# A hybrid convolution and RG-LRU layer: the first projection stage over half of the rows for two sets of seven column tiles, half sums kept in SBUF, and the statistics on two engines

## The chip, the core and the metric

The kernel runs on one core of one Trainium2 chip, in one launch. The metric is the device time of one execution in microseconds (us). Before the change it is 858.16 us, the median of three runs (857.1 to 858.53). PE is TensorE (matmuls), PEld its weight loads, DVE VectorE, ACT ScalarE, POOL GpSimd, and SP the engine that issues the DMAs.

## The reference, cut to what matters

```python
mod_lat = silu(c) @ w_ada + b_ada                  # shift, scale, gate for 512 latent tokens
mod_ctx = silu(c_ctx) @ w_ada + b_ada              # the same for 256 context tokens
hl = rmsnorm(x, norm_g) * (1 + sc_l) + sh_l        # (512, 2048)
hc = rmsnorm(ctx, norm_g) * (1 + sc_c) + sh_c      # (256, 2048)
bl, cl, ul, gl, vl, ql = split(hl @ w_in)          # six blocks of 1024 columns
vc = (hc @ w_in) block v
ya = bl * conv3(cl * ul) * silu(gl)                # rows of 64 tokens
xb = conv4(v) + b_conv_b                           # latent and context
# for both directions: a, b from two block diagonal products and sigmoids of xb,
# h = scan(a, b), the latent scan starting from the last context state
yb = (h_fwd + h_bwd) * silu(ql)
out = rmsnorm(x + gate * (concat(ya, yb) @ w_out), final_g)
```

All of it is float32. The kernel forms a float32 product from three passes: each operand is split into a rounded high part and the remainder (`hi`, `lo`), and `mm3` adds hi*hi, lo*hi and hi*lo.

## The kernel before, in words

The 2048 rows of `w_in` are 16 row tiles (k), its 6144 columns 48 column tiles of 128, named c0, u0, b0, g0 and so on, v0 to v7, q0 to q7. Tokens are the 512 columns of a matmul, and hidden rows are on the partitions.

**Start.** The 16 tiles of x arrive by DMA. ACT squares each one (L211), PE sums the squares over the partitions (L215), with a small matmul of ones behind each from k = 8 on (L218). The sums go through DVE and ACT to 1/rms, which PE transposes over all partitions (L230). `silu_c` (L129) takes a sigmoid on ACT at k = 8. `ada` (L199) multiplies silu(c) with four pieces of `w_ada` for one k; `ada_t` (L236) transposes the result and DVE makes the scale `gs` and shift `sh` of this k; `h_lat` (L252) makes `hi` and `lo` of the hidden row tile.

**First stage (L324).** It goes over all 16 row tiles k; at each k seven column tiles (A_TILES) get their three matmuls each, into seven PSUM banks that stay open for the stage. Between them stand the `ada`, `ada_t` and `h_lat` of the next k, so the stage makes the hidden tiles as it uses them. 2 MB of `w_ada` and 448 KB of `w_in` are loaded for each k.

**Second stage (L584).** A step s takes one half (8 row tiles) of one column tile: 24 matmuls, and 24 narrower ones (256 context tokens) more for a v tile. 82 steps do the other 41 tiles. At its head a step loads the piece for s + 3 and splits that for s + 2 (`split`, L71: `whi` on ACT, then `wlo` on DVE; three buffers each). A finished tile is worked up in the next step (`EV`). Lists by step number (`at`, L516) place all else behind the matmuls of a step: the context's squares and sums (`ctx_sq`, `ctx_stat`, `ctx_stat2`), its hidden tiles (`h_ctx`, L258: product on DVE, `hi` on ACT, `lo` on DVE), the RG-LRU of head tile m in seven steps (`l_prep`, `l_gate`, `l_ix`, `l_exp`, `l_mul`, then `l_sqrt` and `l_scan` in the next seven), the gate `gt_load` and `gt_acc`. Each engine runs its instructions in the order of the code.

**Last stage (L681).** 32 steps multiply y (split by `y_split`, L576) with `w_out`, whose piece DVE first multiplies by the gate (L316), and add x; the final norm ends it.

Of the kernel before, what the change touches and what calls it, by code (L numbers as in the profile page):

```python
# [14 lines left out]
D = 2048  # L15
# [14 lines left out]
for _n, _w in PCOLS:  # L30
# [5 lines left out]
A_TILES = [("c", 0), ("u", 0), ("b", 0), ("g", 0), ("c", 1), ("u", 1), ("b", 1)]  # L36
_REST = [("g", 1)] + [(n, m) for m in range(2, NM) for n in "cubg"]
N_FIRST = 3
BC_TILES = (_REST[:N_FIRST] + [("v", m) for m in range(NM)] + _REST[N_FIRST:]
            + [("q", m) for m in range(NM)])  # L40
NA = len(A_TILES)
W_OFF = {"b": 0, "c": 8, "u": 16, "g": 24, "v": 32, "q": 40}
N_BC = 2 * len(BC_TILES)
N_D = 32
N_GT = 32
NHC = 3
# [3 lines left out]
def tile_hybrid_layer(ctx, tc, xt, ct, xn, wada, wgt, bgt, wa_, wbc, wout, lruw, par, ident, fg, out):  # L50
# [11 lines left out]
    ctx.enter_context(tc.manual_schedule())  # L62
    s_a = ExitStack()
    ta = s_a.enter_context(tc.tile_pool(name="ta", bufs=2))
    pa = ctx.enter_context(tc.tile_pool(name="pa", bufs=6, space=PSUM))
# [96 lines left out]
    aux = pa.tile([128, 512], F32, name="bacc")  # L162
    acc = [pa.tile([128, 512], F32, name="bacc") for i in range(NA - 2)]
    accp = pa.tile([128, 2, 512], F32, name="plru", bufs=1)
    acc += [accp[:, 0, :], accp[:, 1, :]]
# [53 lines left out]
    ssum = ta.tile([128, T], F32, name="sq", bufs=4)  # L219
# [7 lines left out]
    ada(0, 0)  # L227
    ada(0, 1)
# [4 lines left out]
    ada(0, 2)  # L233
    ada(0, 3)
# [23 lines left out]
    def h_ctx(ks):  # L258
        for k in ks:
            nc.vector.scalar_tensor_tensor(xc[k], xc[k], gs[:, k, 1:2], cq["b"], op0=ALU.mult, op1=ALU.mult)  # L260
        for k in ks:
            hctx[k] = (hc.tile([128, TC], F32R, name="xchi", bufs=16 + NHC), hc.tile([128, TC], F32R, name="hclo"))
            nc.scalar.activation(hctx[k][0], xc[k], AF.Identity, bias=sh[:, k, 1:2])
        for k in ks:
# [3 lines left out]
    def ctx_sq(k):  # L268
        t = ta.tile([128, TC], F32, name="sqc", bufs=12) if k else const.tile([128, TC], F32, name="sqc0")
# [6 lines left out]
    def ctx_stat():  # L276
        ps = pa.tile([128, 512], F32, name="bacc")
# [7 lines left out]
    def ctx_stat2():  # L285
        ps = pa.tile([128, 512], F32, name="bacc")
# [5 lines left out]
    def main_a(k, j):  # L292
        hi, lo = wsp["a", k]
        s = slice(128 * j, 128 * j + 128)
        mm3(acc[j], hi[:, s], lo[:, s], hlat[k], T, k == 0, k == KT - 1)


    def piece_src(s):
        if s < N_BC:
            return wbc[s]  # L300
        return wout[s - N_BC]

# [15 lines left out]

    ada_t(0)
    h_lat(0)  # L320
    split_a(0)
    ada(1, 0)
    ada(1, 1)
    for k in range(KT):  # L324
        if k + 2 < KT:
            for p in range(4):
                load_ada(k + 2, p)
            load_wa(k + 2)
        else:
# [464 lines left out]
```

## Time and profile before

| | |
|---|---|
| median of three runs | 858.16 us |
| profiled execution | 858.19 us |
| its span, first to last instruction | 856.4 us |
| PE busy | 838.6 us, 98% |
| DVE, ACT, POOL busy | 493.5 us (58%), 376.6 us (44%), 89.1 us (10%) |
| granted PE clock, mean over the span | 0.993 of full |
| moved by DMA | 136.13 MB |

The span is what the trace covers; 1.8 us of the device time lie outside it. PE's busy time is modelled from its starts, so that the distance from one matmul's start to the next says more than its duration. A row of the timeline has start, duration, engine, line, operation, operands, how many instructions were merged (x), and in brackets how long the engine had been idle and what ended that.

### The profile page before, as it was taken

The page shows a single profiled execution, that of the slowest core. Times are in us where ns is not written, and L with a number is a line of the kernel's source. Part 1 is how long each engine was busy: PE and PEld are TensorE (multiplying, and loading weights), DVE is VectorE, ACT ScalarE, POOL GpSimd, SP SyncE. Part 2 cuts the span into 40 slices and gives each one's busy share as a digit, 9 for nine tenths or more (in the row PEclk, how much of TensorE's full clock was granted, in tenths as well). Part 3 has the DMA queues.
Part 4 walks back from the last instruction along what each step waited for, and adds up shares of the span by engine and source line. Part 5 has one row for each costly group of instructions (what it writes and reads, how often), then busy time and mean ns, then how long its engine had stood idle before and what let it go on. Part 6 is the DMA issues. An engine that isn't in the chain of part 4 may idle for free.

```text
span 856.4 us, 10577 instructions
## 1 busy us (share of the span) xinstructions
PE 838.6 (98%) x4202; PEld 665.3 (78%) x4202; DVE 493.5 (58%) x643; ACT 376.6 (44%) x478; POOL 89.1 (10%) x64
## 2 busy tenths in 40 slices
PE   7899999999999999999999999999999999999996
PEld 1466666888888888878888888887788888888784
DVE  0353434786355446394939585766465777454555
ACT  6322224451111024757576857475846443222234
POOL 0000001600000000202020202120202002020200
PEclk9899999999999999999999999999999999999998
DMA  9899998234222324244435443434223542323204
GB/s 341 341 326 333 352 357 291 103 120 139 82 99 82 116 86 159 99 131 152 143 116 164 145 159 122 161 123 135 74 99 141 204 171 102 120 74 113 84 0 197
DMA packets 41091, 136.13 MB, mean 159 GB/s; under 512 B 4561, under 2 KB 6865, under 8 KB 40401
## 3 DMA queue, kind: packets, MB, share of 16 engines
q1 hardware_dynamic: 41042, 135.46, 44.8%
q8 instruction: 33, 0.54, 0.3%
q14 instruction: 16, 0.13, 0.0%
HBM read 131.24 MB, written 4.19 MB: 158 GB/s over the span
## 4 chain that ended last, share of the span: by engine, by line
PE 93%; DVE 3%; ACT 1%; DMA 1%; issue 1%; SPq 0%; POOL 0%; ACTq 0%; DVEq 0%; POOLq 0%
PE bacc L78 21%; PE bacc L79 20%; PE bacc L80 20%; PE bacc L706 6%; PE bacc L708 6%; PE bacc L707 6%; PE bacc L201 4%; PE plru L78 1%; DMA xhi<-in_xt 1%; PE plru L454 1%; PE plru L79 1%; PE plru L80 1%; PE plru L706 1%; PE plru L708 1%; PE plru L707 1%; PE plru L456 1%
## 5 line engine op out<-in xcount | busy, mean ns | idle before, releaser
L78 PE MATMUL bacc<-xhi,whi 128*128 128x512 f32 x736 | 293.3, 399 | 1.6 <-ACT whi L73 1.6
L74 DVE TENSOR_TENSOR wlo<-raw,whi 128x1024 fp32r<-128x1024 f32 (+1 forms) x130 | 162.2, 1252 | 220.5 <-ACT whi L73 219.3
L79 PE MATMUL bacc<-xhi,wlo 128*128 128x512 f32 x736 | 288.1, 391 | 0.5 <-DVE wlo L74 0.5
L80 PE MATMUL bacc<-hlo,whi 128*128 128x512 f32 x736 | 287.7, 391 | 0.0
L73 ACT CAST whi<-raw 128x1024 fp32r<-128x1024 f32 (+1 forms) x130 | 134.3, 1035 | 246.3 <-PE bacc L80 127.2
L78 PEld LDWEIGHTS bacc<-xhi,whi 128*128 128x128 f32 x736 | 138.5, 188 | 37.2 <-issue 7.5
L80 PEld LDWEIGHTS bacc<-hlo,whi 128*128 128x128 f32 x736 | 138.6, 188 | 30.3
L79 PEld LDWEIGHTS bacc<-xhi,wlo 128*128 128x128 f32 x736 | 138.7, 188 | 28.3 <-DVE wlo L74 1.2
L706 PE MATMUL bacc<-whi,yhi 128*128 128x512 f32 x224 | 87.3, 390 | 0.3 <-DVE xr L639 0.3
L707 PE MATMUL bacc<-wlo,yhi 128*128 128x512 f32 x224 | 87.2, 389 | 0.0
L708 PE MATMUL bacc<-whi,ylo 128*128 128x512 f32 x224 | 87.1, 389 | 0.0
L464 POOL TENSOR_TENSOR li<-li,xb 128x768 f32<-128x768 f32 x16 | 30.9, 1933 | 393.5 <-ACT li L461 393.5
L460 ACT ACTIVATE lr<-plru,pt 64x768 f32<-64x768 f32 x32 | 28.8, 899 | 48.6 <-PE plru L457 41.7
L706 PEld LDWEIGHTS bacc<-whi,yhi 128*128 128x128 f32 x224 | 42.0, 188 | 9.4 <-DVE xr L639 0.8
L708 PEld LDWEIGHTS bacc<-whi,ylo 128*128 128x128 f32 x224 | 42.0, 188 | 8.8
L707 PEld LDWEIGHTS bacc<-wlo,yhi 128*128 128x128 f32 x224 | 42.0, 188 | 8.7
L504 DVE SCALAR_TENSOR_TENSOR gacc<-raw,cs,gacc 128x1024 f32<-128x1024 f32 x32 | 42.5, 1329 | 0.1
L316 DVE TENSOR_TENSOR raw<-raw,gacc 128x1024 f32<-128x1024 f32 x32 | 41.7, 1304 | 0.0
L80 PE MATMUL bacc<-hclo,whi 128*128 128x256 f32 x128 | 36.2, 283 | 0.0
L79 PE MATMUL bacc<-xchi,wlo 128*128 128x256 f32 x128 | 36.2, 283 | 0.0
L78 PE MATMUL bacc<-xchi,whi 128*128 128x256 f32 x128 | 36.1, 282 | 0.0
L201 PE MATMUL bacc<-rada,cs 128*32 128x256 f32 x512 | 35.1, 393 | 0.3 <-DVE mods L242 0.3
(158 smaller groups left out, 859.0 us busy)
## 6 DMA issues: line engine op xcount, KB each, us to landing
raw<-in_wbc SPq DMA_DIRECT2D x82, 512.0 KB, 3.2
rada<-in_wada SPq DMA_DIRECT2D x64, 512.0 KB, 5.7
raw<-in_wgt SPq DMA_DIRECT2D x32, 512.0 KB, 4.3
raw<-in_wout SPq DMA_DIRECT2D x32, 512.0 KB, 3.2
raw<-in_wa_ SPq DMA_DIRECT2D x16, 448.0 KB, 6.9
xhi<-in_xt SPq DMA_DIRECT2D x16, 256.0 KB, 4.9
xr<-in_xn SPq DMA_DIRECT2D x4, 1024.0 KB, 7.2
xchi<-in_ct SPq DMA_DIRECT2D x16, 128.0 KB, 3.7
```

Source lines behind the costliest of these rows:

```text
L73: nc.scalar.copy(hi[:, :n], raw[:, :n])
L74: nc.vector.tensor_tensor(lo[:, :n], raw[:, :n], hi[:, :n].bitcast(F32), op=ALU.subtract)
L78: nc.tensor.matmul(acc, wh, h[0][:, :n], start=first, stop=False, **kw)
L79: nc.tensor.matmul(acc, wl, h[0][:, :n], start=False, stop=False, **kw)
L80: nc.tensor.matmul(acc, wh, h[1][:, :n], start=False, stop=last, **kw)
L201: nc.tensor.matmul(aux[32 * j:32 * j + 32, 0:256], cs[:, 4 * p + j, :], rawa[g, p][:, j, :], start=p == 0, stop=p == 3, skip_group_check=True)
L316: nc.vector.tensor_tensor(r3, r3, g, op=ALU.mult)
L464: nc.gpsimd.tensor_tensor(lru["i", d], lru["i", d], xb[m], op=ALU.mult)
L504: nc.vector.scalar_tensor_tensor(gacc[:, s], gtq.pop(i), cs[:, k, 0:1], gacc[:, s], op0=ALU.mult, op1=ALU.add)
L706: nc.tensor.matmul(accs[t], yh[:, ts], hi[:, w], start=kk == 0, stop=False)
L707: nc.tensor.matmul(accs[t], yh[:, ts], lo[:, w], start=False, stop=False)
L708: nc.tensor.matmul(accs[t], yl[:, ts], hi[:, w], start=False, stop=kk == KT - 1)
```

## The change

The first stage covers only the first eight row tiles, for the same seven column tiles (now P_TILES). Their half sums are then copied out of PSUM into SBUF tiles (`part`), three by DVE and four by ACT. Seven other tiles (Q_TILES: c2, u2, b2, g2, c3, u3, b3) follow in single steps: steps 0 to 6 over the first eight row tiles, with the `ada`, `ada_t` and `h_lat` of k = 9 to 15 between their matmuls, steps 7 to 13 over the last eight. Steps 14 to 29 are the v tiles, steps 30 to 36 the second halves of P_TILES, to which DVE adds the half sums (`ev_part`), steps 37 to 88 the remaining 26 tiles. There are 89 steps for 82 before, and eight long steps of the first stage for 16. The matmuls of the projection are the same in number.

At the start DVE squares the odd x tiles, the matmuls of ones stand in groups (`warm`), all four `ada` of k = 0 come behind the transposes, and the weights of k = 0 are split before its `h_lat`. The context is loaded in step 6, squared in steps 7 to 9, summed at the end of step 10; its hidden tiles are made one at a time. The last LRU scan is in step 87 of 89 (79 of 82 before), and all six first `y_split` in step 88 (80 and 81 before).

```diff
+P_TILES = [("c", 0), ("u", 0), ("b", 0), ("g", 0), ("c", 1), ("u", 1), ("b", 1)]
+Q_TILES = [("c", 2), ("u", 2), ("b", 2), ("g", 2), ("c", 3), ("u", 3), ("b", 3)]
+_REST = ([("g", 1), ("g", 3)] + [(n, m) for m in range(4, NM) for n in "cubg"]
+         + [("q", m) for m in range(NM)])
+STEPS = ([(t, 0) for t in Q_TILES] + [(t, 1) for t in Q_TILES]
+         + [(("v", m), h) for m in range(NM) for h in range(2)]
+         + [(t, 1) for t in P_TILES] + [(t, h) for t in _REST for h in range(2)])
+S_V = 2 * len(Q_TILES)
...
+    def warm(n):
+        for _ in range(n):
+            nc.tensor.matmul(acc[0][:, :128], ones, ones, start=True, stop=True)
...
-        nc.scalar.activation(sq, xl[k], AF.Square)
+        if k % 2:
+            nc.vector.tensor_tensor(sq, xl[k], xl[k], op=ALU.mult)
+        else:
+            nc.scalar.activation(sq, xl[k], AF.Square)
...
-        if k >= 8:
-            nc.tensor.matmul(acc[0][:, :128], ones, ones, start=True, stop=True)
+    warm(3)
...
-    ada(0, 0)
-    ada(0, 1)
+    warm(4)
...
-    ada(0, 2)
-    ada(0, 3)
+    for p in range(4):
+        ada(0, p)
+    warm(2)
...
     ada_t(0)
+    warm(8)
+    split_a(0)
     h_lat(0)
-    split_a(0)
     ada(1, 0)
     ada(1, 1)
...
+    def main_p(k, j):
+        main_a(k, j)
+        if k == KH - 1:
+            part.append(ya.tile([128, T], F32, name="yA"))
+            if j % 2:
+                nc.vector.tensor_copy(part[j], acc[j])
+            else:
+                nc.scalar.copy(part[j], acc[j])
...
-    S_C0 = 2 * (N_FIRST + NM)
+    S_C0 = S_V + 2 * NM
...
-    at(3, h_ctx, range(0, 3))
-    at(4, h_ctx, range(3, 6))
-    at(4, h_ctx, range(6, 9))
-    at(5, h_ctx, range(9, 12))
-    at(5, h_ctx, range(12, 15))
-    at(5, h_ctx, range(15, 16))
+    for k in range(KT):
+        at(NA + k // 6, ctx_sq, k)
+        at(S_V - 3 + k // 6, h_ctx, [k])
+    at(S_V - 4, ctx_stat)
+    at(S_V - 3, ctx_stat2, first=True)
...
     for k in range(6):
-        at(S_Y + k // 3, lambda k=k: y_split(dp1[0], k))
+        at(S_Y, lambda k=k: y_split(dp1[0], k))
...
+    def ev_part(n, m, ps):
+        t = part[P_TILES.index((n, m))]
+        nc.vector.tensor_tensor(t, t, ps, op=ALU.add)
+        if n == "c":
+            cur["c"] = t
+        else:
+            EV[n](m, t)
...
+            if s < NA and k in (1, 3, 6):
+                h_ada(KH + 1 + s, {1: 0, 3: 1, 6: 2}[k])
...
+            if c < 2:
+                sets = (sets if c else []) + [[bank() for _ in range(2 if c else 4)]]
+                if c == 1:
+                    sets[1] += [pair[:, 0, :], pair[:, 1, :]]
+            accs = sets[c % 2]
```

`h_ada(k, j)` is the old `ada(k, 2)`, `ada(k, 3)` for j = 0, `ada_t(k)`, `h_lat(k)` for j = 1, and `ada(k + 1, 0)`, `ada(k + 1, 1)` for j = 2. `bank()` hands out six PSUM banks in turn, as the pool did.

The order on DVE where the context's hidden tiles are made, before: `xchi` is the product, `hclo` the remainder, which needs the `hi` that ACT makes from the product.

```order
L179 TENSOR_TENSOR rq_rc<-rq_rc,rq_uc 128x2
L74 TENSOR_TENSOR wlo<-raw,whi 128x1024
L260 SCALAR_TENSOR_TENSOR xchi<-xchi,gs,rinvC 128x256 x3
L265 SCALAR_TENSOR_TENSOR hclo<-xchi,sh 128x256 x3
L74 TENSOR_TENSOR wlo<-raw,whi 128x1024
L504 SCALAR_TENSOR_TENSOR gacc<-raw,cs,gacc 128x1024
L260 SCALAR_TENSOR_TENSOR xchi<-xchi,gs,rinvC 128x256 x3
```

The products stand in threes, so that ACT can work on the first while DVE makes the next. The same place on DVE now, in steps 11 and 12, with the numbers of the tiles:

```order
L531 SCALAR_TENSOR_TENSOR gacc_1349<-raw_1521,cs_132,gacc_1349 128x1024
L277 SCALAR_TENSOR_TENSOR xchi_1256<-xchi_1256,gs_161,rinvC_1572 128x256
L284 SCALAR_TENSOR_TENSOR hclo_1577<-xchi_1256,sh_162,xchi_1576 128x256
L277 SCALAR_TENSOR_TENSOR xchi_1258<-xchi_1258,gs_161,rinvC_1572 128x256
L284 SCALAR_TENSOR_TENSOR hclo_1583<-xchi_1258,sh_162,xchi_1582 128x256
L277 SCALAR_TENSOR_TENSOR xchi_1260<-xchi_1260,gs_161,rinvC_1572 128x256
```

Each remainder now stands right behind its own product; six such pairs stand between one `wlo` and the next (steps 11 and 12), four more behind that of step 13.

The order on DVE at the end of the second stage, before: `lt` to `xb` (L486 to L492) is the last scan, `sgt` and `xb` (L395, L396) the gate of a q tile, `raw` the multiplication of a `w_out` piece, `ylo` the split of y.

```order
L395 TENSOR_TENSOR sgt<-sgt,bacc 128x512
L396 TENSOR_TENSOR xb<-xb,sgt 128x512
L74 TENSOR_TENSOR wlo<-raw,whi 128x1024
L486 TENSOR_TENSOR lt<-lt,li 128x768
...
L492 TENSOR_TENSOR xb<-li 128x512
L316 TENSOR_TENSOR raw<-raw,gacc 128x1024
L74 TENSOR_TENSOR wlo<-raw,whi 128x1024
L395 TENSOR_TENSOR sgt<-sgt,bacc 128x512
L396 TENSOR_TENSOR xb<-xb,sgt 128x512
L580 TENSOR_TENSOR ylo<-yA,yhi 128x512 x3
```

Behind the scan stand the piece of the last stage's first step and the gate of q6. The same place now:

```order
L335 TENSOR_TENSOR raw<-raw,gacc 128x1024
L87 TENSOR_TENSOR wlo<-raw,whi 128x1024
L423 TENSOR_TENSOR sgt<-sgt,bank_86 128x512
L424 TENSOR_TENSOR xb<-xb,sgt 128x512
L513 TENSOR_TENSOR lt<-lt,li 128x768
...
L519 TENSOR_TENSOR xb<-li 128x512
L335 TENSOR_TENSOR raw<-raw,gacc 128x1024
L87 TENSOR_TENSOR wlo<-raw,whi 128x1024
L612 TENSOR_TENSOR ylo<-yA,yhi 128x512 x6
L423 TENSOR_TENSOR sgt<-sgt,bank_87 128x512
```

The scan has moved behind the gate of q6 and behind the first piece of the last stage, and the six splits behind the second piece.

## Rows read from the trace of the kernel before

**Rows 1.** The page's first section: busy us, share of the span, instructions, by engine.
```profile
PE 838.6 (98%) x4202; PEld 665.3 (78%) x4202; DVE 493.5 (58%) x643; ACT 376.6 (44%) x478; POOL 89.1 (10%) x64
```

**Rows 2.** What PE waited for: us in total, times, longest us.
```profile
PE plru L454 <- ACT li L461: 0.5, 1, 0.5
...
PE bacc L706 <- DVE xr L639: 0.3, 1, 0.3
```

**Rows 3.** Stretches of the start: busy us of each engine, granted clock, DMA.
```profile
30.00:31.00 1.00, 0.28 (x8) 0.00 (x0) 0.27 (x1) 0.70 (x2) 0.00 (x0) 1.00 0.95 340
...
34.00:36.00 2.00, 2.00 (x17) 0.60 (x16) 0.00 (x0) 0.00 (x0) 0.00 (x0) 0.50 0.96 390
```

**Rows 4.** The chain that ended last, at the start: start us, us, what.
```profile
15.02 0.97 PE plru L215 x2
15.99 0.42 PE bacc L218 x2
```

**Rows 5.** The timeline of the start.
```profile
12.75 0.23 ACT L130 ACTIVATE sg<-pt 128x32 f32<-128x32 f32 x1
...
23.00 0.69 DVE L220 COPY sq<-plru 128x512 f32<-128x512 f32 x1 [9.64 <-PE plru L215]
...
26.88 1.07 PE L201 MATMUL bacc<-rada,cs 128*32 128x256 f32 x16
...
28.44 0.44 PE L239 MATMUL bacc<-idt,sada 128*128 128x128 f32 x2 [0.49 <-ACT sada L205]
...
29.52 0.75 DVE L247 SCALAR_TENSOR_TENSOR xhi<-xhi,gs,rinvB 128x512 f32<-128x512 f32 x1
...
31.90 0.65 PE L78 MATMUL bacc<-xhi,whi 128*128 128x512 f32 x1 [1.62 <-ACT whi L73]
...
43.07 0.40 PE L78 MATMUL bacc<-xhi,whi 128*128 128x512 f32 x1
```

**Rows 6.** The timeline of DVE while the context's hidden tiles are made, and after.
```profile
174.28 1.28 DVE L260 SCALAR_TENSOR_TENSOR xchi<-xchi,gs,rinvC 128x256 f32<-128x256 f32 x3 [1.21 <-ACT rinvC L290]
...
190.56 0.48 DVE L260 SCALAR_TENSOR_TENSOR xchi<-xchi,gs,rinvC 128x256 f32<-128x256 f32 x1
191.67 0.48 DVE L265 SCALAR_TENSOR_TENSOR hclo<-xchi,sh 128x256 fp32r<-128x256 f32 x1 [0.64 <-ACT xchi L263]
...
193.76 0.68 DVE L380 TENSOR_TENSOR cutile<-ctile,bacc 128x512 f32<-128x512 f32 x1
...
196.43 1.28 DVE L504 SCALAR_TENSOR_TENSOR gacc<-raw,cs,gacc 128x1024 f32<-128x1024 f32 x1
```

**Rows 7.** The timeline of ACT at the same place.
```profile
191.13 0.51 ACT L263 ACTIVATE xchi<-xchi,sh 128x256 fp32r<-128x256 f32 x1 [1.06 <-DVE xchi L260]
191.54 1.04 ACT L73 CAST whi<-raw 128x1024 fp32r<-128x1024 f32 x1
```

**Rows 8.** The timeline of PE there: first matmuls of steps 4, 6 and 7.
```profile
173.54 0.48 PE L78 MATMUL bacc<-xhi,whi 128*128 128x512 f32 x1
...
184.52 0.39 PE L78 MATMUL bacc<-xhi,whi 128*128 128x512 f32 x1
...
192.83 0.40 PE L78 MATMUL bacc<-xhi,whi 128*128 128x512 f32 x1
```

**Rows 9.** The timeline of DVE at the end of the second stage.
```profile
659.93 0.95 DVE L486 TENSOR_TENSOR lt<-lt,li 128x768 f32<-128x768 f32 x1
...
666.22 1.22 DVE L316 TENSOR_TENSOR raw<-raw,gacc 128x1024 f32<-128x1024 f32 x1
668.69 1.23 DVE L74 TENSOR_TENSOR wlo<-raw,whi 128x1024 fp32r<-128x1024 f32 x1 [1.25 <-ACT whi L73]
...
671.93 1.89 DVE L580 TENSOR_TENSOR ylo<-yA,yhi 128x512 fp32r<-128x512 f32 x3
```

**Rows 10.** The timeline of ACT there.
```profile
667.60 1.05 ACT L73 CAST whi<-raw 128x1024 fp32r<-128x1024 f32 x1 [9.14 <-DVE raw L316]
...
676.08 1.66 ACT L579 CAST yhi<-yA 128x512 fp32r<-128x512 f32 x3
```

More of the change, by code (lines that the diff above doesn't have):

```diff
@@ L62, in tile_hybrid_layer, with bank @@
     ctx.enter_context(tc.manual_schedule())
+    ya = ctx.enter_context(tc.tile_pool(name="ya", bufs=9))
     s_a = ExitStack()
     ta = s_a.enter_context(tc.tile_pool(name="ta", bufs=2))
-    pa = ctx.enter_context(tc.tile_pool(name="pa", bufs=6, space=PSUM))
+    pa = ctx.enter_context(tc.tile_pool(name="pa", bufs=1, space=PSUM))
+    single = [pa.tile([128, 512], F32, name=f"bank{i}") for i in range(6)]
+    pair = pa.tile([128, 2, 512], F32, name="pair")
+    turn = [5]
+    def bank():
+        turn[0] += 1
+        return single[(turn[0] - 1) % 6]
     def raw_tile():
@@ L159, in softplus @@
         nc.vector.tensor_scalar(nsp8, w0, -LRU_C, None, op0=ALU.mult)
[L162 to L165, printed above, removed]
+    aux = single[5]
+    acc = single[:5] + [pair[:, 0, :], pair[:, 1, :]]
     cq = {}
@@ L276, in ctx_stat @@
     def ctx_stat():
-        ps = pa.tile([128, 512], F32, name="bacc")
+        ps = bank()
         for j in range(2):
@@ L285, in ctx_stat2 @@
     def ctx_stat2():
-        ps = pa.tile([128, 512], F32, name="bacc")
+        ps = bank()
         for j in range(2):
@@ L412, in ev_v @@
     def ev_v(m, ps, psc):
[L413 removed]
+        t = xbp.tile([128, TA], F32, name="xb")
         xb[m] = t
@@ L506, in gt_sum @@
     def gt_sum(j):
-        p = pa.tile([128, 512], F32, name="bacc")
+        p = bank()
         s = slice(512 * j, 512 * j + 512)
@@ L583, in tile_hybrid_layer @@
     load_piece(2)
-    for s in range(N_BC):
-        ti, half = divmod(s, 2)
-        n, m = BC_TILES[ti]
+    for s, ((n, m), half) in enumerate(STEPS):
+        if s < NA - 1:
+            for p in range(4):
+                load_ada(KH + 2 + s, p)
+        if s == NA - 1:
+            for k in range(KT):
+                load_xc(k)
+        if s == NA:
+            s_a.close()
+            xbp = ctx.enter_context(tc.tile_pool(name="xbp", bufs=8, reuse_waits="tile"))
+            gp = ctx.enter_context(tc.tile_pool(name="gp", bufs=1, reuse_waits="tile"))
+            tq[0] = s_c.enter_context(tc.tile_pool(name="tcx", bufs=1, reuse_waits="tile"))
+            gacc = gp.tile([128, D], F32, name="gacc")
+            nc.gpsimd.memset(gacc, 0.0)
         if s + 3 < NS:
@@ L596, in tile_hybrid_layer @@
             split_piece(s + 2)
-        for _ in range(min(len(evq), 4 if s == 0 else 2)):
-            evq.pop(0)()
         hi, lo = wsp.pop(s)
-        if half == 0:
-            accs[ti] = [pa.tile([128, 512], F32, name="bacc")]
-            if n == "v":
-                accs[ti].append(pa.tile([128, 512], F32, name="bacc"))
-        for k in range(8):
+        t = (n, m)
+        if t in Q_TILES:
+            accs[t] = [acc[Q_TILES.index(t)]]
+        elif t not in accs:
+            accs[t] = [bank(), bank()] if n == "v" else [bank()]
+        new = half == 0 or t in P_TILES
+        for k in range(KH):
             if k == 4:
```

137 lines of the change are left out of this document (64 added, 73 removed).

## The prediction

> **What bounds the kernel now.** I read the busy times first: TensorE (PE) is at work for 838.6 of 856.4 us and no other engine for more than 58% [rows 1]. So the time is PE's own work plus the places where PE waits. The list of PE's waits comes second: behind the start it has only two entries worth a tenth, 0.5 us for a gate of the RG-LRU and 0.3 us in the last stage [rows 2]. The timeline of the start comes third: the first matmul of the first stage stands at 31.90 and the first of its second row tile at 43.07 [rows 5], 11.2 us for a step whose work is 7.4 us (21 matmuls at 0.229, which is 10.98 us for the 48 between steps 4 and 6 [rows 8], two times 1.07 for `ada` [rows 5], 0.44 for the transposes [rows 5]). Fourth, the stretches show why: PE was busy for 0.28 of the microsecond from 30 to 31 and ran at a granted clock of 0.50, 1.2 of its 2.4 GHz, from 34 to 36 [rows 3]. The change leaves the matmuls of the projection, of `ada` and of the last stage as many as they were. What it can gain is at the start; what it can lose is any place where PE now waits for VectorE (DVE) or ScalarE (ACT), which work in the order of the code. The rest is a search for such places.
>
> The profiled execution took 858.19 us, 0.03 above the median, so the sum against it is a sum against the median.
>
> **The start.** Each sum of squares costs PE 0.97, each pair of ones behind it 0.42 [rows 4]. DVE could copy the sums at 23.00 [rows 5]. Now the square of k = 9 is DVE's and stands behind the work on the sigmoid, which ACT begins at 12.75 for 0.23 [rows 5]; with 0.4 us for the small operations there and at most 0.75 for a square (the 512-wide product at 29.52 [rows 5] is the nearest row), it is there at 14.1. Seven sums without ones follow, 6.8 us: 20.9, a gain of 2.1. From the copy to the end of the transposes it was 3.9 us (23.00 to 26.88 [rows 5]); three and four pairs of ones now stand in that way and are longer than the DVE work beside them by 0.5 and 0.2: 25.5. Then all of `ada` for k = 0, two times 1.07, and two pairs of ones, 0.84: the transposes of `ada_t` begin at 28.45, where they began before (28.44 [rows 5]). So the gain of the squares is spent. Behind it DVE splits the first weights (1.1, as 896 of the 1024 columns that take 1.23 [rows 9]) before it makes the product that used to start at 29.52; that product is done at 31.4 and ACT's `hi` 0.7 later, 32.1. PE meanwhile has 0.44 of transposes, eight pairs of ones, 3.4, and `ada`, 1.07: its first matmul of the stage comes at 33.3, 1.4 later than before. But PE has then not been idle since 14, so I take the full clock, and both weight parts are there: the second row tile begins at 33.3 + 7.4 = 40.7 in place of 43.07. Gain 2.4. Bounds: 3.5 if ones in a row are cheaper (the first matmul then waits for `hi` at 32.1), a loss of 1.4 if the clock falls all the same and the step takes 11.2 again.
>
> **The first stage in two sets.** Eight steps of 7.4 and seven with 24 matmuls and the same `ada` (8.1) replace sixteen. The loads per step are 2.5 and 2.6 MB in a longer step, so DMA has more room, not less. Seven copies out of PSUM (0.7 each, the copy of 23.00 [rows 5]) lie under the next step; the seven additions lie under single steps. The context's squares and sums end about 4 us before PE needs them. I cost all this at nothing; if the copies' cover were gone it would be 0.7 once, for the first bank.
>
> **The context's hidden tiles.** This is the largest term. A lone one is in the trace: product at 190.56, remainder at 191.67 [rows 6], between them ACT's `hi` at 191.13 for 0.51 [rows 7]. The next DVE instruction may start 0.40 later (three products take 1.28, one 0.48 [rows 6]), so one after another costs 1.51 per tile. Before, with three products side by side, three tiles took 2.4.
> Call 0 the first product; it started 0.74 behind step 4's first matmul (174.28 against 173.54 [rows 6, 8]), and now does behind step 12's. Step 14 begins 10.24 (10.98 less 0.74) and step 15 another 8.31 later (184.52 to 192.83 [rows 8]).
> - Six tiles (0 to 5). ACT can start the weights of step 14 0.98 behind the sixth product (191.54 against 190.56 [rows 6, 7]), at 7.55 + 0.98 = 8.53; 1.04 for `whi`, 1.23 for `wlo` [rows 9]: 10.83. PE's second matmul of step 14 wants it at 10.47. Late by 0.4.
> - DVE goes on at 10.75 with six more: `whi` of step 15 at 19.28, `wlo` done at 21.58. Step 15, already 0.4 late, wants it at 10.24 + 0.4 + 8.31 + 0.23 = 19.18. Late by 2.4.
> - Then the u3 tile's convolution, 2.67 (193.76 to 196.43 [rows 6]), and `gt_acc`, 1.2, stand before the last four tiles: they start at 25.4, the fourth product at 29.9, its remainder is done at 31.5. Step 15's latent half ends at 26.85, and the context part takes 0.35 per row tile, so row tile 15 is wanted at 29.5. Late by about 1.9.
> - The weights of step 16 stand behind that on both engines: `wlo` at 33.15, wanted at 31.8. Late by 1.35.
> Sum 6.1. Behind each waiting DVE instruction stands the next `wlo`, and for that PE waits. Bounds: nothing, if a tile costs the 0.8 of the threes; 8, if each costs 0.1 more.
>
> **The RG-LRU.** The 0.5 us of [rows 2] comes where a u tile's convolution stands right ahead of the scan of head tile 0. Now u4 stands so ahead of the scan of head tile 1, and u1 and b1, with an addition each, ahead of that of head tile 0. I take 0.5 and 0.7 for these, so 0.7 more than before; bounds 0 and 2.
>
> **The end of the second stage.** Before, the last scan began at 659.93 and its followers at 666.22, 6.29 us [rows 9]. It did not wait for a gate, and the splits of y were ready before the last stage. Now it stands behind the gate of q6. Step 87's first matmul is 0: ACT starts `whi`, table and sigmoid; from that `whi` to the end of DVE's gate it is 4.33 (667.60 to 671.93 [rows 9, 10]). Scan until 10.6; multiplied piece, 1.38 to ACT's `whi` (666.22 to 667.60 [rows 9, 10]), 12.0; `wlo` starts 1.09 later (668.69) and ends at 14.3; the first `ylo` 0.63 later (three take 1.89 [rows 9]), 14.9. The last stage could begin at 10.98 (two steps). Its first matmul needs `yhi` (1.05 and 0.55 behind 12.0 [rows 10]): 13.6, late by 2.6; its third needs `ylo`: 0.9 more. Sum 3.5; bounds 0 (as before) and 4.5.
>
> **The last stage.** The fourth column group now takes other banks than the third, so the wait of 0.3 [rows 2] goes: the banks are long free.
>
> Sum: 858.2 - 2.4 + 6.1 + 0.7 + 3.5 - 0.3 = 865.8 us, 0.9% slower.
>
> **Rivals.**
> 1. Occupancy decides, not order: the waits of PE don't arise. For it: DVE is busy 58%, ACT 44% [rows 1], and in steps 12 to 15 DVE has some 24 us of work in 28 us. The point is the price of a context tile: two groups of six and two splits must end by 18.8, so a tile may cost 1.28 and no more. Against it: the only lone tile costs 1.51, and engines that wait for each other in turn are half idle at that. The waits at the last stage would go by the same mechanism, if the gate of q6 came as early as the scan of before. Time 858.2 - 2.4 - 0.3 = 855.5: faster. Chance 9%.
> 2. Only the wait at the last stage fails to come, or most of it: the gate may be ready earlier than in the row, where ACT was itself late. 862.3. Chance 13%. The mirror of it, that only the context's waits stay away, is 859.7: 4%.
> 3. The start brings nothing: the clock falls again, or the ones are in the way. 865.8 + 2.4 to 3.8, so 868 to 869.6. For it: PE's first matmul is later than before. Against it: PE has no idle stretch like that of 30 to 31 [rows 3]. Chance 8%.
> 4. PE's idle time before the last stage lets the clock fall. At the start a stretch of about 4 us, whose emptiest part is in [rows 3], preceded some 6 us at 0.50, which cost 3.1 us of work. The waits here, 2.6 and 0.9 with work around them, are shorter: 868.9. Chance 6%.
> The Trainium skill ("TensorE: Matmul & The Clock Gate", Part 1 on the HAM clock gate) says that the array's clock is given by its recent activity, and that it has only the half and the full state; idle time throttles it again. The trace agrees on both levels (0.50 and 1.00 in [rows 3]). By that rule the ones at the start are worth their time, and the new waits before the last stage are a risk, which is this rival.
>
> **How the numbers follow.** The forecast has 60%, and its own range is 863 to 868.5. What a measurement of this kernel can tell from no change is about 0.2%, 1.7 us. Faster than 856.4: rival 1, and a little for a start that gives more, 10%. Within: the mirror of rival 2 and parts of rival 1, 6%. Slower: the rest, 84%. The range that leaves out no more than 2 in 10 goes from 860 (most of rival 2) to 869.5 (rivals 3 and 4).
>
> **What would show it.** In the profile after: the second row tile's first matmul near 40.7 and no granted clock of 0.50 behind 30; among PE's waits, entries for `wlo` and the context's `hi` and remainder of some 6 us together in steps 14 to 16, with DVE and ACT in turn; entries for `yhi` and `ylo` of some 3.5 us at the first step of the last stage, right behind the last scan; the 0.3 of the last stage gone. I am wrong if PE runs without a gap through steps 14 to 16, or if the last scan begins before the gate of q6.

## The result and the profile after

The changed kernel takes 870.97 us (median of 4 runs, 870.39 to 872.46), the kernel before beside it 858.09 us. The ratio is 1.0154, 95% interval 1.0137 to 1.0172: 1.5% slower. Forecast were 865.8 us and a range of 860 to 869.5, so the direction was right and the size was not: the time lies above the range. The profiled execution took 870.39 us, its span 868.6 us, 12.2 more than before.

Busy times after, in the columns of [rows 1]:

```profile
PE 839.7 (97%) x4220; PEld 668.3 (77%) x4220; DVE 506.4 (58%) x660; ACT 373.6 (43%) x470; POOL 87.2 (10%) x64
```

PE is busy for 1.1 us more, so 11 of the 12.2 us are idle time. What it waits for, after (columns of [rows 2]; the left-out rows are at the start):

```profile
PE bank L755 <- ACT yhi L611: 5.9, 1, 5.9
...
PE pair L481 <- ACT li L488: 3.0, 2, 2.5
PE bank L92 <- DVE wlo L87: 1.5, 2, 0.8
...
PE pair L91 <- DVE yA L363: 1.4, 1, 1.4
PE bank L91 <- ACT whi L86: 1.2, 1, 1.2
PE pair L755 <- DVE xr L687: 0.8, 1, 0.8
```

The distances from one step's first matmul to the next, before and after, give the account by stage. One step of 5.44 us stands ahead of the v tiles now that stood behind them before; it is set off between the second row and the last.

| stage | forecast, us | measured, us |
|---|---|---|
| start, to the second row tile | -2.4 | -8.4 (34.69 for 43.07) |
| first stage in two sets | 0 | +2.1 |
| context tiles (the first three v steps, 14 to 16) | +6.1 | +6.1 |
| the other 13 v steps | 0 | -1.0 |
| gates of the RG-LRU | +0.7 | +4.4 |
| begin of the last stage | +2.6 | +6.1 |
| its first step | +0.9 | +2.6 |
| later in the last stage | -0.3 | +0.5 |
| the rest | 0 | -0.3 |

**The start.** PE and DVE there, after (timeline, columns of [rows 5]):

```profile
13.02 3.78 PE L233 MATMUL pair<-yA,ones 128*32 128x512 f32 x14 [1.47 <-DVE yA L227]
16.83 0.69 DVE L237 COPY yA<-pair 128x512 f32<-128x512 f32 x1 [1.14 <-PE pair L233]
23.41 1.95 PE L222 MATMUL bank<-ones 128*128 128x128 f32 x16
26.78 0.50 PE L91 MATMUL bank<-xhi,whi 128*128 128x512 f32 x1 [0.41 <-ACT xhi L265]
34.69 0.40 PE L91 MATMUL bank<-xhi,whi 128*128 128x512 f32 x1
```

Seven sums (14 instructions) take 3.78 us, 0.54 each; the row of 0.97 had been used for them [rows 4]. Eight pairs of ones take 1.95 and not 3.4. The copy stands at 16.83 for 23.00 [rows 5]. The start differs a little from one execution to the next: in the profiles of the other runs with this start the second row tile begins at 34.98 to 35.90.

**The context tiles.** DVE, ACT and PE at steps 14 to 16 (timeline):

```profile
185.59 0.48 DVE L277 SCALAR_TENSOR_TENSOR xchi<-xchi,gs,rinvC 128x256 f32<-128x256 f32 x1
186.17 0.51 ACT L280 ACTIVATE xchi<-xchi,sh 128x256 fp32r<-128x256 f32 x1 [1.01 <-DVE xchi L277]
186.71 0.48 DVE L284 SCALAR_TENSOR_TENSOR hclo<-xchi,sh 128x256 fp32r<-128x256 f32 x1 [0.64 <-ACT xchi L280]
187.11 0.48 DVE L277 SCALAR_TENSOR_TENSOR xchi<-xchi,gs,rinvC 128x256 f32<-128x256 f32 x1
...
192.66 1.03 ACT L86 CAST whi<-raw 128x1024 fp32r<-128x1024 f32 x1
...
193.74 0.50 PE L91 MATMUL bank<-xhi,whi 128*128 128x512 f32 x1 [1.19 <-ACT whi L86]
195.00 0.50 PE L92 MATMUL bank<-xhi,wlo 128*128 128x512 f32 x1 [0.76 <-DVE wlo L87]
```

A lone tile takes 1.52 us (185.59 to 187.11; forecast 1.51 from [rows 6, 7]), and the weights of step 15 stand behind the sixth such tile of their group. The three steps take 10.06, 11.63 and 9.44 us, where the later v steps of this kernel take 8.27 and those of before 8.34.

**Head 1 of the RG-LRU.** PE waits 2.54 us for `li`, since the scan of head 0, which reads the old `li`, is late on DVE (timeline):

```profile
364.87 0.69 DVE L408 TENSOR_TENSOR cutile<-yA 128x512 f32<-128x512 f32 x1
...
367.55 0.95 DVE L504 SCALAR_TENSOR_TENSOR lt<-lx,lt 128x768 f32<-128x768 f32 x1
370.15 0.96 DVE L504 SCALAR_TENSOR_TENSOR lt<-lx,lt 128x768 f32<-128x768 f32 x1 [1.65 <-POOL lx L503]
...
378.51 0.95 DVE L513 TENSOR_TENSOR lt<-lt,li 128x768 f32<-128x768 f32 x1
...
385.86 0.50 PE L481 MATMUL pair<-xs,lwh 128*128 128x512 f32 x1 [2.54 <-ACT li L488]
```

DVE first works up u1 (from 364.87), then waits 1.65 us for POOL: `lx` has one buffer, so POOL squares the second half only when DVE has used the first. Behind PE's wait the clock is at half (stretch):

```profile
388.00:390.00 2.00, 2.00 (x6) 1.56 (x5) 2.00 (x2) 1.32 (x2) 0.58 (x1) 0.50 0.26 102
```

**Before the last stage** (timeline, and the stretches in the columns of [rows 3]: us, busy of PE, PEld, DVE, ACT, POOL, granted clock, DMA):

```profile
665.43 0.96 DVE L504 SCALAR_TENSOR_TENSOR lt<-lx,lt 128x768 f32<-128x768 f32 x1 [1.65 <-POOL lx L503]
...
667.45 1.22 DVE L335 TENSOR_TENSOR raw<-raw,gacc 128x1024 f32<-128x1024 f32 x1
668.74 1.05 ACT L86 CAST whi<-raw 128x1024 fp32r<-128x1024 f32 x1 [1.47 <-DVE raw L335]
...
671.74 0.69 DVE L423 TENSOR_TENSOR sgt<-sgt,bank 128x512 f32<-128x512 f32 x1 [0.68 <-ACT sgt L422]
...
673.07 0.95 DVE L513 TENSOR_TENSOR lt<-lt,li 128x768 f32<-128x768 f32 x1
...
679.35 1.22 DVE L335 TENSOR_TENSOR raw<-raw,gacc 128x1024 f32<-128x1024 f32 x1
...
682.35 0.80 PE L755 MATMUL bank<-whi,yhi 128*128 128x512 f32 x1 [5.92 <-ACT yhi L611]
```

```profile
680.00:682.00 2.00, 0.00 (x0) 0.00 (x0) 0.76 (x2) 1.27 (x2) 0.00 (x0) 0.56 1.01 414
682.00:684.00 2.00, 1.53 (x3) 0.81 (x4) 2.00 (x3) 2.00 (x5) 0.00 (x0) 0.50 0.99 418
684.00:686.00 2.00, 2.00 (x6) 1.54 (x6) 2.00 (x5) 1.39 (x3) 0.00 (x0) 0.50 0.82 250
```

The order is the forecast's (gate of q6, scan 6.28 long, multiplied piece); but the scan begins 7.68 us behind step 87's first matmul (665.39), 3.35 more than the 4.33 forecast, and PE's clock falls in the wait.

### The profile page after: what moved, and what is told of

It is laid out like the page before. It is cut to its first block, busy times and chain, and to the rows that moved or that the text cites. A ratio compares the mean times of both kernels' runs of the same rounds, so it can differ in the third digit from the quotient of the medians.

```text
span 868.6 us, 10583 instructions
## 1 busy us (share of the span) xinstructions
PE 839.7 (97%) x4220; PEld 668.3 (77%) x4220; DVE 506.4 (58%) x660; ACT 373.6 (43%) x470; POOL 87.2 (10%) x64
## 4 chain that ended last, share of the span: by engine, by line
PE 84%; DVE 8%; ACT 4%; issue 1%; DMA 1%; POOL 0%; SPq 0%; ACTq 0%; DVEq 0%; POOLq 0%
PE bank L91 18%; PE bank L93 18%; PE bank L92 18%; PE bank L757 5%; PE bank L756 5%; PE bank L755 5%; PE bank L212 4%; PE pair L755 2%; PE pair L756 2%; PE pair L757 2%; DVE wlo L87 1%; PE pair L91 1%; DMA xhi<-in_xt 1%; ACT whi L86 1%; PE pair L481 1%
## 5 line engine op out<-in xcount | busy, mean ns | idle before, releaser
L91 PE MATMUL bank<-xhi,whi 128*128 128x512 f32 x720 | 288.0, 400 | 1.6 <-ACT whi L86 1.2
L92 PE MATMUL bank<-xhi,wlo 128*128 128x512 f32 x720 | 282.4, 392 | 1.7 <-DVE wlo L87 1.5
L93 PE MATMUL bank<-hlo,whi 128*128 128x512 f32 x720 | 282.3, 392 | 0.1
L91 PEld LDWEIGHTS bank<-xhi,whi 128*128 128x128 f32 x720 | 135.7, 189 | 38.1 <-issue 8.1
L93 PEld LDWEIGHTS bank<-hlo,whi 128*128 128x128 f32 x720 | 136.0, 189 | 30.6 <-DVE hlo L266 0.9
L92 PEld LDWEIGHTS bank<-xhi,wlo 128*128 128x128 f32 x720 | 136.1, 189 | 29.5 <-DVE wlo L87 2.7
L755 PE MATMUL bank<-whi,yhi 128*128 128x512 f32 x192 | 75.7, 394 | 5.9 <-ACT yhi L611 5.9
L757 PE MATMUL bank<-whi,ylo 128*128 128x512 f32 x192 | 75.6, 394 | 0.1
L756 PE MATMUL bank<-wlo,yhi 128*128 128x512 f32 x192 | 75.4, 393 | 0.0
L755 PEld LDWEIGHTS bank<-whi,yhi 128*128 128x128 f32 x192 | 36.6, 191 | 13.9 <-ACT yhi L611 6.3
```

What stands on the lines that cost most here:

```text
L91: nc.tensor.matmul(acc, wh, h[0][:, :n], start=first, stop=False, **kw)
L92: nc.tensor.matmul(acc, wl, h[0][:, :n], start=False, stop=False, **kw)
L93: nc.tensor.matmul(acc, wh, h[1][:, :n], start=False, stop=last, **kw)
L755: nc.tensor.matmul(accs[t], yh[:, ts], hi[:, w], start=kk == 0, stop=False)
L756: nc.tensor.matmul(accs[t], yh[:, ts], lo[:, w], start=False, stop=False)
L757: nc.tensor.matmul(accs[t], yl[:, ts], hi[:, w], start=False, stop=kk == KT - 1)
```

## The experiments

Ratios are to the kernel before, run beside it on the same chip, with the 95% interval in brackets; 0.001 is 0.86 us. Each run has one profiled execution, from which the steps and waits are read. Theory A is that each wait sits where an instruction stands behind others in an engine's order, and can be removed there; the rivals are named with each.

**1. Context tiles in threes again.**

```diff
-        at(S_V - 3 + k // 6, h_ctx, [k])
+    for g in range(6):
+        at(S_V - 3 + g // 2, h_ctx, range(3 * g, min(3 * g + 3, KT)))
-NHC = 2
+NHC = 3
```


> The changed kernel with the context's hidden tiles made in threes again (six groups, two each in steps 11 to 13, one more buffer), nothing else. Theory A (order: PE waits where a weight split is queued behind hand-overs between VectorE and ScalarE): the first three v steps, now 10.06, 11.63 and 9.43 us, come down to 8.3 each, the clock stays full there, and the time is 871.0 - 6.3 = 864.7. Theory B (the first stage in two sets is what costs, and its lateness shows up wherever the next wait is): the waits move to another place, and the time stays above 869.

863.8 us, ratio 1.0067 [1.0050, 1.0084]. The three v steps take 8.27 us each, 6.3 less together, and the waits for `whi` and `wlo` are gone. The term of 6.1 was right. The profiled span shrinks by 7.8, to 860.8: step 40 takes 8.96 us for 10.56, since the clock stayed at 1.00 there behind the same wait for `li` (first matmul behind it, and the stretch):

```profile
380.00 0.50 PE L481 MATMUL pair<-xs,lwh 128*128 128x512 f32 x1 [2.53 <-ACT li L488]
```

```profile
380.00:382.00 2.00, 2.00 (x10) 1.70 (x11) 1.52 (x4) 1.95 (x3) 0.00 (x0) 1.00 0.34 115
```

**2. The last scan one step earlier, the splits of y over two steps.**

```diff
-    at(S_C0 + 7 * NM + 1, l_scan, NM - 1)
+    at(S_C0 + 7 * NM, l_scan, NM - 1)
-        at(S_Y, lambda k=k: y_split(dp1[0], k))
+        at(S_Y + k // 3, lambda k=k: y_split(dp1[0], k))
```


> The changed kernel with the last scan put into step 86 behind its square roots, ahead of the gate of q6, and the first six splits of y shared between steps 87 and 88; nothing else. Theory A (order): the scan starts near 667.5 in place of 673.1; the piece of the last stage's first step then stands behind it, so its first matmul is late by about 3 us instead of 6.1, and if the clock no longer falls another 2.6 come back: 865 to 868. Theory B (DVE simply has too much work at the end): the last stage begins as late as now, 870.5 or more.

867.69 us, 1.0112 [1.0097, 1.0127]. The wait for `yhi` falls from 5.9 to 2.1 us, so the order was the cause of most of it. The clock still falls there, behind this wait and one of 0.8 us for `ylo`: the first step of the last stage takes 8.31 us.

**3. The start alone, on the kernel before.** The diff is that of the start in the change.

> The kernel before with the new start alone: squares on two engines, the matmuls of ones in groups, all four products of the first row tile's modulation behind the transposes, its weights split before its hidden tile. First stage, second stage and all else as before. Theory A: the start is independent of the first stage, the second row tile begins near 34.7 in place of 43.07, and the time is 858.1 - 8.4 = 849.7. Theory B (the first stage in two sets is what makes the early start possible, because sixteen steps of 7.47 us with 2.5 MB each would outrun DMA): steps of the first stage grow beyond 7.47, and the time is 853 to 857.

851.15 us, 0.9918 [0.9904, 0.9933]: faster than both kernels. The second row tile begins at 35.90. The steps of the first stage stay at 7.47 us, but for the third (7.90), so the loads do not need the second set of tiles.

**4. Its parts.** The ones in a row, squares as before:

```diff
-        if k >= 8:
-            nc.tensor.matmul(acc[0][:, :128], ones, ones, start=True, stop=True)
+    for _ in range(8):
+        nc.tensor.matmul(acc[0][:, :128], ones, ones, start=True, stop=True)
```


> The kernel before with only one thing of the new start: the eight matmuls of ones stand in a row behind the last sum of squares and no longer behind each sum from k = 8 on. Theory A: the change of stationary operand between a sum and the ones is what made a sum and its ones take 1.39 us (14.95 to 16.34, seven times); in a row the sums follow ScalarE's squares at 0.57 us, 7 times 0.82 or 5.7 us earlier, and the eight ones then cost 1.95: 3.8 us less, second row tile near 39.3, 854.2 us. Theory B: ScalarE's squares set that pace and the gain of the new start comes from VectorE's share of them; then this stays within 0.5 us of 858.

The odd squares on DVE, ones as before:

> The kernel before with only the odd squares on VectorE, the ones still behind each sum. Theory A: a sum and its ones keep their 1.39 us on TensorE, so the squares are early and nothing comes of it: within 0.5 us of 858. Theory B: the squares were the bound; the sums end some 4 us earlier and the time is about 853 us.

852.78 us, 0.9943 [0.9926, 0.9960], and 858.19 us, 1.0003 [0.9993, 1.0014]. With the ones in a row (timeline):

```profile
13.44 4.16 PE L215 MATMUL plru<-sq,ones 128*32 128x512 f32 x14 [1.02 <-ACT sq L211]
17.53 2.05 PE L218 MATMUL bacc<-ones 128*128 128x128 f32 x16
17.64 0.69 DVE L220 COPY sq<-plru 128x512 f32<-128x512 f32 x1 [4.39 <-PE plru L215]
...
37.48 0.40 PE L78 MATMUL bacc<-xhi,whi 128*128 128x512 f32 x1
```

With the squares shared and the ones between, a sum and its ones keep their pace:

```profile
13.72 1.04 PE L218 MATMUL plru<-sq,ones 128*32 128x512 f32 x2 [1.05 <-DVE sq L212]
14.69 0.49 PE L221 MATMUL bacc<-ones 128*128 128x128 f32 x2
15.11 1.04 PE L218 MATMUL plru<-sq,ones 128*32 128x512 f32 x2
```

1.39 us from sum to sum against 0.59 in a row. So the matmuls of ones between the sums were most of what the start lost. The other edits of run 3 add some 2 us (by the ratios), and not by an earlier first matmul (28.01 in run 3, 27.48 with the ones in a row): the step of the first row tile takes 7.89 us in run 3, and 10.01 with the ones in a row, where the clock was at half. The stretch with the ones in a row, and then in run 3:

```profile
30.00:32.00 2.00, 2.00 (x18) 0.86 (x11) 0.00 (x0) 0.38 (x1) 0.00 (x0) 0.50 1.02 405
```

```profile
30.00:32.00 2.00, 2.00 (x17) 1.43 (x10) 1.33 (x3) 0.87 (x2) 0.00 (x0) 1.00 1.02 408
```

Which of those other edits keeps the clock up was not tried. The sums use 32 columns of the array (128*32), the ones all 128. The Trainium skill (TensorEngine Tiling (Array Packing), Key Properties) says that changing the tiling mode drains TensorE. These two runs agree with it, with 0.5 us a turn (1.39 less 0.59 and 0.26 for the two apart); that it is the mode and not the change of weights alone was not tried.

**5. The old start on the changed kernel.** The start's lines of the change undone.

> The changed kernel with the start of the kernel before (all squares on ScalarE, a matmul of ones behind each sum from k = 8, `ada` around the transposes, `h_lat` ahead of the split). Theory A: the start gives 8.4 us to whatever follows, so this is 871.0 + 8.4 = 879.4 us, with the second row tile near 43.1. Theory B: a later start gives the loads more lead, and part of the 8.4 us comes back behind it (the alone-run start gained only 6.6 us in the median): 877.6 us.

878.39 us, 1.0247 [1.0227, 1.0268], 8.0 us above the change by ratio; in the profiled spans it is 5.8 (874.4 for 868.6). The profiled execution was the fastest of the four (876.21 to 879.56): the step of its first row tile took 10.07 us, where that of before took 11.16, and its second row tile begins at 41.44 for 43.07. The two theories were 1.8 us apart, and these numbers do not part them.

**6. Two buffers for `lx`** (`name="lx", bufs=2`).

> The changed kernel with two buffers for `lx` in place of one, so that POOL makes the second square while VectorE still uses the first. Theory A: the late gates of head 1 and the late last scan both rest on VectorE's 1.65 us wait for that second square, once behind u1 and once behind b7. Then PE's wait for `li` falls from 2.5 to about 0.9 us and the wait for `yhi` from 5.9 to about 4.3 us; 871.0 less 1.65 twice is 867.7 us, and about 866.3 if the half clock behind the first of these waits goes too. Theory B: VectorE's own work in front of the scans (an addition and a convolution) is what makes them late, and POOL's square is only one of several things that are ready too late; the waits stay within 0.5 us of what they were: 870.5 us or more.

869.04 us, 1.0140 [1.0125, 1.0155]. DVE no longer waits between the halves:

```profile
370.54 1.82 DVE L504 SCALAR_TENSOR_TENSOR lt<-lx,lt 128x768 f32<-128x768 f32 x2
```

The wait for `li` falls to 1.8 and that for `yhi` to 4.5 us, where 0.9 and 4.3 were expected: POOL's square is a part of both. The step of head 1 shrinks by 2.25 us, for the clock stays at 1.00 there. The time shows only 1.2 us of it (see 8).

**7. The tiles before the scan of head 0 in another order.** First c1, u1, b1, c0, u0, b0, g0:

```diff
-         + [(t, 1) for t in P_TILES] + [...
+         + [(t, 1) for t in P_TILES[4:] + P_TILES[:4]] + [...
```


> The changed kernel with steps 30 to 36 in the order c1, u1, b1, c0, u0, b0, g0 in place of c0, u0, b0, g0, c1, u1, b1: the additions of b0 and the gate of g0 now stand ahead of head 0's scan, where u1's convolution (four VectorE instructions, 2.7 us) and b1 stood. Theory A: the late scan of head 0 (378.51) and with it PE's wait for `li` of 2.5 us and the half clock behind it come from that place in the order. The scan then starts 2 us or more earlier, the wait falls under 0.5 us, the step of 10.56 us to 6.2 to 6.8, and the time to about 867 us. Theory B: POOL's second square (1.65 us) alone decides; the wait for `li` stays at 1.5 us or more, and the time within 1.5 us of 871.

872.43 us, 1.0166 [1.0142, 1.0190], and PE's wait grew to 3.9 us: neither theory. ACT shows why (timeline):

```profile
372.98 0.63 ACT L422 ACTIVATE sgt<-yA 128x512 f32<-128x512 f32 x1 [4.88 <-DVE yA L593]
373.63 1.28 ACT L508 ACT_TABLE_LOAD   x1
374.92 1.58 ACT L508 ACTIVATE lt<-lt 128x768 f32<-128x768 f32 x2
```

The sigmoid of g0 now stood ahead of head 0's square roots and waited for an addition that DVE makes behind its own wait for POOL; then the table of the square root had to be loaded, which in the changed kernel is loaded while ACT waits. With b0 and b1 there and g0 early (c0, u0, g0, c1, u1, b0, b1):

> The changed kernel with steps 30 to 36 in the order c0, u0, g0, c1, u1, b0, b1: the two steps ahead of head 0's scan work up u1 and b0 no longer beside the squares and the scan; what stands there is b0 and b1 (1.4 us each on VectorE), and no sigmoid of ScalarE, which the order c1, u1, b1, c0, u0, b0, g0 had put into the chain of the square root. Theory A: u1's convolution there (3.4 us with its addition) is what is late: head 0's scan starts 2 us earlier than at 378.5, PE's wait for `li` falls from 2.5 to about 0.5 us, the step from 10.6 to 8.0 or less, and the time to about 868 us. Theory B: the 1.65 us wait of VectorE for POOL's second square is the whole cause; the wait for `li` stays at 2 us or more and the time at 871.

868.0 us, 1.0116 [1.0099, 1.0133]. The wait is 0.47 us, the step 6.91 for 10.56. Its DVE rows show that the reason given was only partly right:

```profile
371.08 0.96 DVE L504 SCALAR_TENSOR_TENSOR lt<-lx,lt 128x768 f32<-128x768 f32 x1 [1.65 <-POOL lx L503]
...
379.44 0.95 DVE L513 TENSOR_TENSOR lt<-lt,li 128x768 f32<-128x768 f32 x1
```

This execution's steps lie 3.0 us later (383.44 for 380.44), so the scan at 379.44 is 2.1 us earlier against them. The 1.65 us for POOL are still there: moving u1 and doubling `lx` are two ways to the same wait.

**8. The two-bank PSUM tile.** One half of `pair` was read while PE was to write the other: by the copies of half sums, and in the last stage.

```diff
-        if k == KH - 1:
+        if k == KH - 1 and j != 5:
+            for i in ([5, 6] if j == 6 else [j]):
...
-                    sets[1] += [pair[:, 0, :], pair[:, 1, :]]
+                    sets[1] = [pair[:, 0, :], sets[1][0], pair[:, 1, :], sets[1][1]]
```


> The changed kernel in which the two half sums of the two-bank PSUM tile are copied only when both are complete, and the fourth column group of the last stage takes its banks in the order pair, single, pair, single. Theory A: PE's waits of 1.4 us (half sum copy) and 0.8 us (last stage) come from reading one half of a tile while PE is to write the other half. Then both go, less about 0.4 for the step that follows: 871.0 less 1.8 to 2.5, 868.5 to 869.2 us. Theory B: they are waits for the bank itself, which is copied too late; they stay at 1 us or more under the same line or the next, and the time is within 0.6 us of 871.0.

870.45 us, 1.0157 [1.0139, 1.0175]. Both waits are gone from the trace (the step of 9.12 us takes 7.69), and the time does not show it. The step after gives 0.5 back, and step 16, the third v step, takes 11.04 us for 9.44. The stretches of this kernel there, and then those of the changed one:

```profile
196.00:198.00 2.00, 2.00 (x11) 1.65 (x10) 1.97 (x3) 0.00 (x0) 0.00 (x0) 1.00 0.53 217
...
208.00:210.00 2.00, 2.00 (x7) 1.52 (x6) 2.00 (x2) 0.00 (x0) 0.00 (x0) 0.50 0.72 256
```

```profile
196.00:198.00 2.00, 2.00 (x6) 1.60 (x5) 1.93 (x4) 0.00 (x0) 0.00 (x0) 0.50 0.75 254
...
208.00:210.00 2.00, 2.00 (x11) 1.64 (x10) 2.00 (x3) 0.00 (x0) 0.00 (x0) 1.00 0.79 248
```

Among the context's waits the clock falls in step 15 (the changed kernel, 2), in step 16 (6, both of 7, 8 and the second of 9), or in neither (5 and the first of 9). In step 15 it costs nothing (11.63 with, 11.63 without): the context tiles set that step's end. In step 16 it costs 1.6 us: 11.0 in those five profiled executions, 9.4 in the other four with lone context tiles, among them kernels that are the same up to there. So a gain of 1.5 us elsewhere can be lost in this place from one execution to the next.

**9. Ones in the wait before the last stage.** First 44, then 23 matmuls:

```diff
+        if q == 0:
...
+            for _ in range(44):
+                nc.tensor.matmul(spare[:, :128], ones, ones, start=True, stop=True)
```


> The changed kernel with 44 matmuls of ones, 0.12 us each at the full clock, between the last step of the second stage and the last stage: about 5.3 us of PE work in the 5.9 us in which it waits for `yhi`. Theory A: the first step of the last stage takes 8.0 us in place of 5.4 only because PE's clock fell in that wait. Then the granted clock stays at 1.00 through 680 to 688 and the time is 871.0 less 2.6, 868.4 us. Theory B: that step is long because its operands come late (yhi, ylo, wlo in turn); the time stays 871, or is more by the ones that are not done when `yhi` is there.

872.38 us, 1.0180 [1.0165, 1.0196]. The clock stayed full and the first step took 5.55 us, but the price of the ones was wrong by a factor of two (0.12 us is an instruction, and a float32 matmul has two). They ended some 3.7 us after the stage could have begun:

```profile
676.78 9.99 PE L749 MATMUL bank<-ones 128*128 128x128 f32 x88
686.52 0.48 PE L760 MATMUL bank<-whi,yhi 128*128 128x512 f32 x1
```

> The changed kernel with 23 matmuls of ones before the last stage, at 0.227 us each as they took there with 44 (9.99 us): 5.2 us of the 5.9 us wait. Theory A: the clock then stays full and the ones are done when `yhi` is there: the first step of the last stage starts where it did and takes 5.5 in place of 8.0 us: 871.0 - 2.5 = 868.5 us. Theory B: the clock falls behind the last short gap all the same, or the ones delay the step: 870.5 us or more.

870.61 us, 1.0150 [1.0135, 1.0165]. In the trace the clock is 1.00 in every stretch from 678 to 688, and the step takes 6.46 us for 8.04:

```profile
684.28 0.50 PE L760 MATMUL bank<-whi,yhi 128*128 128x512 f32 x1 [0.78 <-ACT yhi L611]
...
685.62 0.50 PE L762 MATMUL bank<-whi,ylo 128*128 128x512 f32 x1 [0.61 <-DVE ylo L612]
```

So of the 2.6 us the clock is 1.6, and late operands 1.0. The time does not show the 1.6; step 16 took 11.0 us in the profiled execution.

**10. Everything mended at once** (1, 2, 6, the second order of 7, and 8).

> The changed kernel with every found cause mended at once: context tiles in threes, the last scan a step earlier and the splits of y spread, half sums and bank order of the two-bank tile, two buffers for `lx`, and steps 30 to 36 in the order c0, u0, g0, c1, u1, b0, b1. Theory A: the two sets cost nothing of themselves, what was lost is waits; with the wait for `li` (1.6 us at 854.4) gone too it comes to 852.5 us, and within 1.5 us of the 851.15 of the kernel before with the new start. Theory B: something of the two sets stays (copies, additions, a clock that falls elsewhere): 854 us or more.

851.79 us, 0.9933 [0.9918, 0.9948], with the step of head 1 at 6.18 us. The same without 6 and with the old order of tiles, but with DVE's first half of the LRU's product ahead of a tile's work-up, was tried first:

> The changed kernel with four orders mended: context tiles in threes, the last scan in step 86, the copies of the two halves of the PSUM pair both behind the second half's matmuls and the fourth column group of the last stage taking pair and single banks in turn, and the first half of the multiplication of the RG-LRU ahead of a tile's working up. Theory A: 871.0 - 6.3 (context) - 1.4 and 1.1 (pair) - 3 to 5.5 (scan) - 1 to 3 (multiplication) = 854 to 858, no slower than the kernel before. Theory B: gains do not add up, 864 or more.

854.41 us, 0.9956 [0.9940, 0.9973], with 1.6 us of the wait for `li` left. So the two sets, once their waits are mended, end within 0.6 us of the new start alone (1.3 by the ratios, and the intervals overlap): they bring nothing. But this kernel has two mends that run 3 has not, the buffers of 6 and the bank order of 8; run 11 is the like for like.

**11. A version that beats both.** The kernel before with the new start, two buffers for `lx`, and the fourth column group on the banks of the second:

> The kernel before with the new start, two buffers for `lx`, and the fourth column group of the last stage on the two banks that the second one used, in the order pair, single, pair, single. Theory A: the two waits that are left in that kernel (0.75 us in the step of head 1's second gate, 0.62 in the first step of the fourth group) go: 851.15 - 1.4 = 849.8 us. Theory B: neither edit reaches what is waited for, or the steps behind give the time back: 851 us.

849.17 us, 0.9897 [0.9881, 0.9914]: 1.0% faster than before, and all waits over 0.3 us that are left are at the start. The two waits it was to remove are gone from its trace.

Against it the first kernel of run 10 is 2.6 us slower (3.1 by the ratios, and the intervals do not overlap), so the two sets do cost something. The two profiles are 2.3 us apart. By their steps, 2.9 us are lost around the begin of the last stage, where PE still waits 0.7 us for `yhi`, 0.8 for `ylo` and 0.5 for `wlo`, and 0.9 in the first stage; the v steps (8.27 for 8.34) and the start give 1.6 back. That the RG-LRU now has 59 steps between the v tiles and the last stage, and had 60, may be why its end is still late; no run tried another order.

## Why the prediction was wrong, by its own steps

Four terms were wrong in size, in both directions. The waits were costed too short, in the RG-LRU, at the last stage and in the two sets; the start gained more than was forecast. That the sum missed by some 5 us and not by 10 is luck.

- **"Each sum of squares costs PE 0.97, each pair of ones 0.42"** failed. Both rows were read where the two stand in turn. In a row they cost 0.54 and 0.24, so "the gain of the squares is spent" and the later first matmul fell with it. The term of -2.4 measured -8.4: the sums are 3.0 us shorter than forecast, DVE's square is there 1.1 earlier (13.02 for 14.1), the way from the copy to the first matmul is 2.4 shorter, and the first row tile's step 0.5 longer (7.91). Its bound (a gain of 3.5) kept the 0.97 for the sums. That PE, not idle since 14, would have the full clock was right.
- **"I cost all this at nothing" (the two sets)** failed by 2.1 us. A bound of 0.7 for the copies was there, but not that a copy of one bank holds back matmuls into the other bank of the same tile (1.37 us; run 8). Run 8 gives 0.9 of the 2.1 back, net of 0.5 in the step behind; no run takes the rest away. The same mechanism put 0.8 us into the last stage, where the forecast had a wait go. The old wait of 0.3 did go.
- **The context's tiles** were right in mechanism and sum: 1.51 forecast and 1.52 measured for a tile, 6.1 and 6.1 for the whole; run 1 takes it away. The waits in the list (2.7 us) are only part of it; the rest is waits too short for the list, and work at the half clock that is hidden behind the tiles.
- **The RG-LRU** failed in size: 0.7 forecast, bound 2, measured 4.4. The step saw that u1 and b1 stand ahead of the scan, and priced it by the 0.5 us of [rows 2], a case in which slack had taken most. DVE's queue was not added up: with 3.4 us for u1 and 1.65 for POOL the scan is so late that PE waits 2.5 us, and the clock fell in that wait too. Runs 6 and 7 show both parts of the wait, run 1 that 1.6 us of the step are the clock (8.96 for 10.56 with the same wait).
- **The begin of the last stage** was right in order, wrong in one assumption: "Step 87's first matmul is 0: ACT starts `whi`". ACT starts it 3.35 us later (668.74 for 665.39), since it waits for DVE's multiplied piece (667.45), and DVE was behind by then, from head 7's products with their wait for POOL and the gate of q5 before them. From that `whi` to the end of the gate it is 4.33, as in the row. Forecast 2.6, measured 5.9, and the difference is these 3.35. Run 2 takes back most of the wait, run 6 1.4 us of it.
- **Rival 4** (the clock falls in that wait), given 6%, came true: 1.6 us of the first step's 2.6, the rest being late operands (0.9 forecast, 1.0 measured). It had been held down because the waits were costed too short.
- Rivals 1 to 3 did not come. The range failed on the high side: the gain at the start was 6.0 us larger than forecast, and the terms against it together 10.6 us larger (20.6 for 10.0).

## What to carry to other kernels

Read a price from a row in the same neighbourhood: an instruction that alternates with another form can cost twice what it costs in a row. Where a change adds work ahead of a chain, add up that engine's whole queue from the last point where it was idle, with its waits for a third engine; a wait of 0.5 us in the old trace is what slack left over, not a price. And before a restructuring is kept for its gain, run its parts alone: here moving the ones at the start carried most of the gain (5 of 7 us), and the restructuring, with every wait mended that was found, still ended 2.6 us behind the same mends without it (10 and 11).

## What the runs showed of the hardware

- Summing matmuls on 32 columns with full-width ones between took 1.39 us a turn, against 0.59 for the sum in a row (runs of 4).
- The granted clock fell to 0.50 behind PE's waits of 5.9 us and of 2.5 us (head 1, changed kernel), and stayed at 1.00 behind 1.8 us (run 6) and 0.5 us (second of 7). Behind the same 2.5 us it stayed at 1.00 in run 1, and in run 2 it fell behind 2.1 and 0.8 us close together. Among the shorter waits of the context tiles the place where it fell changed between executions.
- A function table came between two ACT functions at 1.28 us, with the next instruction right behind it (373.63 to 374.92, first of 7).
